# Layer 1's modulation as two-column products on TensorE beside the last attention heads

## The chip, the cores and the metric

One core of a Trainium2 chip. The metric is the device time of one execution in microseconds: 2973.62 us, the median of 3 runs (2972.55 to 2975.34). The engines are TensorE (PE, with its weight loads as PEld), VectorE (DVE), ScalarE (ACT), GpSimd (POOL) and SyncE (SP), which issues all DMAs of this kernel.

## What is computed

Two layers of a trunk over 1024 prompt tokens and 64 sample tokens, 1024 features. Layer 0 mixes with retention and differential attention, layer 1 with band attention and a state-space scan; each layer ends in a gated feed-forward network. What the change touches is the modulation: six vectors of 1024 values per layer and sequence (two sequences, prompt and sample), which scale, shift and gate the rest.

```python
c_act = jax.nn.silu(c)
for l in range(DEPTH):
    mod = c_act @ w_mod[l] + b_mod[l]                 # 1024 x 6144 per layer, fp32
    sh1, sc1, g1, sh2, sc2, g2 = jnp.split(mod, 6)    # one pair of columns: prompt, sample
    h = rmsnorm(x, norm_g[l, 0]) * (1.0 + sc1) + sh1
    ...                                               # attention and retention or scan -> out
    x = x + g1 * out
    h = rmsnorm(x, norm_g[l, 1]) * (1.0 + sc2) + sh2
    ...                                               # feed-forward -> f
    x = x + g2 * f
```

## The kernel before

The program is written in Tile: a planner orders each engine's instructions from the order of the program (earlier ones have priority) and its own model of when they are ready; pools hand out buffers by tag. The large products use fp32r, two halves (hi, lo) of each operand, three products each, and the stages follow one another: layer 0's projections and heads (to about 660 us), output product and norm, up products with the gate (line L648, about 799 to 1228), down products (L804, 1228 to 1513), then the same of layer 1 (heads to about 2140, up 2259 to 2683, down from 2683).

A layer's modulation is cut into 24 units of 256 output columns. Units 0 to 3 are the shift, 4 to 7 the scale and 8 to 11 the gate of the first half of the layer, 12 to 23 the same for the feed-forward half. Each has 1 MB of weights. Layer 0's units are made at the start and beside its retention. Layer 1's units are made by `mod_steps1` (L440): per unit four loads of 256 KB (L447), 16 ACT products (L453) that scale 128x256 weights with a per-partition value, 7 DVE sums of 128x512 (L455), then in `mod_sum` (L409) four transposes on TensorE and a DVE reduction (L411). Units 0 to 6 run in the up products of layer 0, from column block `f` = 4 on (the fifth of 22), where each block makes two of the five steps of a unit; units 7 to 19 in the down products of layer 0, one step each 1.6 tiles, with the rest finished ahead of the last pass; units 20 to 23 in the up products of layer 1. The class `Modulation` counts these steps. In the up products the side work's tiles (`mh`) come from the same 8 buffers as the tiles of the gate.

In the heads, `weave` (L1175) runs one head's attention and, between its steps, steps of `fill` (the projection of the next head, or in the last head the output product on the first half of the features, `early_out`, L1437) and of `side`. The last head of each layer first issues the loads of the output weights (`load_cols`, L188) and of the finished heads (`load_mixed`, `mxl`, L1575), then its attention. These loads, the projections' weights and all later weights use one tag `raw` with two buffers; the split halves have two buffers each as well (`wsp`). The products' banks `gs` are two, shared by projections, `early_out` and the first tiles of the next stage. The rest of the side work is finished after the last head, and then comes `block_tail` with the output products (`ops`) on the second half of the features, the norm, and the feed-forward network.

`nps` (L297) is a sum of squares over the partitions by TensorE, from `rstd_bcast`: for each of 3 column groups, 2 products of a 128x128 fp32 block with one column of ones.

Of the kernel before, what the change touches and what calls it, by code (L numbers as in the profile page):

```python
# [50 lines left out]
FS = 1.6  # L51
MHB = 3
MU = (7, 20, 24)
NPRE = 8
MS0 = 4
# [87 lines left out]
def build(ctx, tc, A, O, stop=None):  # L143
# [296 lines left out]
    def mod_steps1(l, units, pp, stage):  # L440

        for u in units:
            src = mod_src(l, u)
            acc = None
            for j0 in range(0, KT, 2):
                rv = stage()[:, :512].rearrange("p (j n) -> p j n", n=256)
                SY.dma_start(out=rv, in_=src[:, j0:j0 + 2, :])  # L447
                yield
                acc = acc or sm.tile([P, 2, 256], F32, tag="macc", name="macc", bufs=1)
                for j in range(j0, j0 + 2):  # L450
                    pr = acc if j == 0 else stage()[:, :512].rearrange("p (j n) -> p j n", n=256)
# [229 lines left out]
    def ffn_up(l, hv, pp, w, tmp, side, last):  # L681
# [12 lines left out]
        for f in range(NF):  # L694
# [33 lines left out]
            if f >= MS0:  # L728
                side.step()
# [33 lines left out]
            if f >= MS0:  # L763
                side.step()
# [28 lines left out]
    def ffn_down(l, x, gate, pp, yp, before, after, side, part0, xres):  # L793
        def tile(js, c, m, parts):
# [22 lines left out]
            side.step()  # L817

        for js in PASSES:
            if js[-1] == NPAIR - 1:  # L820
                before()
# [796 lines left out]
    for h in range(4):  # L1618
# [14 lines left out]
        weave(diff_attention(h, qk_.pop(h), vv_.pop(h), *late), iter(()) if late else fill, DW[h], mside, MS[1])  # L1633
# [5 lines left out]
    mod_scale(0, 1)  # L1639
    sta.close()  # L1640

    def block_tail(l, wout, am, nxt, side, wts):
# [4 lines left out]
        with ExitStack() as st:  # L1647
# [22 lines left out]
            with ExitStack() as su:  # L1670
# [3 lines left out]
                side.start(mod_steps1(1, range(MU[0]) if l == 0 else range(MU[1], MU[2]), pp, lambda: w("mh", F32)), 1)  # L1674
# [4 lines left out]
                ffn_up(l, hv, pp, w, lambda: up_.tile([P, 512], F32, tag="s2", name="s2", bufs=1), side, last)  # L1679
# [14 lines left out]
        def before():  # L1694
            side.end()
            if l == 0:
                mod_scale(1, 0)
                mod_scale(1, 1)
# [540 lines left out]
```

## Time and profile before

| | us |
|---|---|
| median of 3 runs | 2973.62 |
| the profiled execution | 2973.83 |
| its span, first to last instruction | 2972.1 |
| TensorE products busy | 2804.1 (94%) |
| TensorE weight loads busy | 2707.4 (91%) |
| VectorE busy | 1954.3 (66%) |
| ScalarE busy | 1296.3 (44%) |
| GpSimd busy | 787.3 (26%) |
| mean granted TensorE clock | 0.979 |

The span is 2972.1 us; what lies around it is 1.7 us. Busy time of TensorE's products is modelled and overlaps, so the share of its weight loads is the better measure of its idle time. Time runs from the span's start in all views. PEclk is the granted share of full clock, so 0.5 is 1.2 GHz and 1.0 is 2.4 GHz.

### The profile page before, as it was taken

How to read it: one execution, taken by the hardware profiler on the slowest of the kernel's cores; microseconds unless marked ns; L12 is line 12 of the kernel's file. 1: busy time of each engine (PE TensorE's matmuls, PEld its weight loads, DVE VectorE, ACT ScalarE, POOL GpSimd, SP SyncE). 2: the span in 40 equal slices, each digit the busy share in tenths (PEclk: the TensorE clock that was granted, in tenths of full speed). 3: DMA queues.
4: the chain of work that ended last, by engine and by line, in shares of the span. 5: the costliest groups of instructions: out<-in, count | busy, mean ns of one | idle time of the engine just before them, and what ended most of it. 6: DMA issues, size and time to landing. Idle time of an engine off the chain costs nothing.

```text
span 2972.1 us, 51195 instructions
## 1 busy us (share of the span) xinstructions
PE 2804.1 (94%) x19418; PEld 2707.4 (91%) x19418; DVE 1954.3 (66%) x4095; ACT 1296.3 (44%) x2938; POOL 787.3 (26%) x842
## 2 busy tenths in 40 slices
PE   7999999889999999999988999997999999999998
PEld 4999998779899999999988998986998999999997
DVE  5788766654788666587876675456268888764544
ACT  4221265644535444555552335556255454334111
POOL 4332222222255444412342352111100000004131
PEclk9999999889999999999989999999999999999999
DMA  7444421135544333553422331113344533235221
GB/s 241 139 131 142 126 62 60 46 98 159 158 130 137 91 101 96 183 173 128 138 82 74 86 98 50 52 55 93 99 132 144 153 101 102 71 98 184 90 81 61
DMA packets 351069, 330.53 MB, mean 111 GB/s; under 512 B 24898, under 2 KB 307047, under 8 KB 350823
## 3 DMA queue, kind: packets, MB, share of 16 engines
q1 hardware_dynamic: 350823, 327.26, 35.7%
q8 instruction: 153, 2.51, 0.4%
q14 instruction: 93, 0.76, 0.1%
HBM read 248.46 MB, written 78.73 MB: 110 GB/s over the span
## 4 chain that ended last, share of the span: by engine, by line
PE 47%; DVE 9%; DMA 6%; ACT 4%; issue 2%; POOL 1%; SPq 0%; DVEq 0%; ACTq 0%; POOLq 0%
PE dps L804 10%; PE pa L648 7%; PE pe L648 6%; PE pb L648 6%; DMA mh<-in_w_mod 3%; PE py L648 3%; PE qkps L231 3%; PE pvps L2110 2%; DMA raw<-in_w_up 2%; DVE macc L455 1%; ACT mh L453 1%; PE ops L231 1%; PE xps L231 1%; DVE wlo L596 1%; PE ptps L1316 1%
## 5 line engine op out<-in xcount | busy, mean ns | idle before, releaser
L804 PE MATMUL dps<-y,whi 128*128 128x384 f32 (+1 forms) x2112 | 518.8, 330 | 5.9 <-DVE sthi L160 4.2
L804 PEld LDWEIGHTS dps<-y,whi 128*128 128x128 f32 x2112 | 376.0, 189 | 7.2 <-DVE sthi L160 4.7
L595 ACT CAST whi<-raw 128x512 fp32r<-128x512 f32 x328 | 194.7, 617 | 372.4 <-PE pb L648 95.0
L804 PE MATMUL dps<-y,wlo 128*128 128x384 f32 (+1 forms) x1056 | 347.1, 330 | 0.0
L199 POOL TENSOR_TENSOR wlo<-raw,whi 128x2048 fp32r<-128x2048 f32 (+2 forms) x40 | 180.7, 4518 | 373.5 <-ACT whi L198 290.3
L160 DVE SCALAR_TENSOR_TENSOR x<-dps,modT,x 128x384 f32<-128x384 f32 (+1 forms) x320 | 149.4, 495 | 110.7 <-PE dps L804 110.1
L596 POOL TENSOR_TENSOR wlo<-raw,whi 128x512 fp32r<-128x512 f32 x116 | 162.1, 1402 | 208.1 <-ACT whi L595 203.1
L648 PE MATMUL pe<-row,whi 128*128 128x272 f32 x1056 | 205.9, 288 | 0.0
L804 PEld LDWEIGHTS dps<-y,wlo 128*128 128x128 f32 x1056 | 199.7, 189 | 0.0
L596 POOL TENSOR_TENSOR y<-y 128x544 fp32r<-128x544 f32 x88 | 133.0, 1543 | 250.4 <-ACT y L595 250.4
L453 ACT ACTIVATE mh<-mh,cact 128x256 f32<-128x256 f32 x336 | 145.8, 498 | 120.9 <-DMA mh<-in_w_mod 105.8
L455 DVE TENSOR_TENSOR macc<-macc,mh 128x512 f32<-128x512 f32 x168 | 142.7, 849 | 76.9 <-ACT mh L453 64.9
L596 DVE TENSOR_TENSOR wlo<-raw,whi 128x512 fp32r<-128x512 f32 x212 | 148.4, 718 | 64.1 <-ACT whi L595 63.4
L648 PE MATMUL pa<-row,whi 128*128 128x272 f32 x896 | 174.7, 292 | 10.3 <-ACT gs L669 10.3
L231 PE MATMUL qkps<-hhi,whi 128*128 128x384 f32 (+1 forms) x528 | 178.6, 342 | 3.3 <-DVE q L1383 2.0
L231 PE MATMUL qkps<-hlo,whi 128*128 128x384 f32 (+1 forms) x528 | 173.5, 332 | 0.0
L648 PEld LDWEIGHTS pe<-row,whi 128*128 128x128 f32 x1056 | 165.9, 188 | 0.0
L648 PE MATMUL pb<-bt,whi 128*128 128x272 f32 x816 | 156.8, 288 | 1.1 <-DVE u L717 1.1
L648 PE MATMUL pa<-bt,whi 128*128 128x272 f32 x768 | 151.0, 292 | 5.0 <-DVE row L160 3.1
L648 PEld LDWEIGHTS pa<-row,whi 128*128 128x128 f32 x896 | 143.1, 192 | 11.0 <-ACT gs L669 11.0
L648 PE MATMUL pe<-row,wlo 128*128 128x272 f32 x528 | 152.4, 289 | 0.0
L648 PE MATMUL py<-bt,whi 128*128 128x272 f32 x704 | 136.1, 290 | 4.0 <-ACT whi L595 2.4
(462 smaller groups left out, 8077.2 us busy)
## 6 DMA issues: line engine op xcount, KB each, us to landing
raw<-in_w_up SPq DMA_DIRECT2D x104, 512.0 KB
mh<-in_w_mod SPq DMA_DIRECT2D x96, 256.0 KB
yd<-e SPq DMA_DIRECT2D x88, 272.0 KB
y<-yd SPq DMA_DIRECT2D x44, 544.0 KB
raw<-in_w_down SPq DMA_DIRECT2D x22, 1024.0 KB
mq<-in_w_mod SPq DMA_DIRECT2D x64, 256.0 KB
raw<-in_w_in_ab SPq DMA_DIRECT2D x24, 512.0 KB
xr<-xspill SPq DMA_DIRECT2D x32, 193.0 KB
```

Of the source, the lines that this page charges most:

```text
L160: V.scalar_tensor_tensor(out=out, in0=in0, scalar=scalar, in1=in1, op0=op0, op1=op1, **kw)
L199: eng.tensor_tensor(out=lo[:, sl], in0=raw[:, sl], in1=hi[:, sl].bitcast(F32), op=ALU.subtract)
L231: T.matmul(out=ps[:, b:n], lhsT=lt, rhs=rh, start=(i == 0), stop=(i == len(mms) - 1))
L453: S.activation(out=pr[:, s, :], in_=rv[:, j - j0, :], func=AF.Copy, scale=cact[:, j, s:s + 1])
L455: V.tensor_add(acc, acc, pr)
L595: S.copy(hi, src)
L596: eng.tensor_tensor(out=lo, in0=src, in1=hi.bitcast(F32), op=ALU.subtract)
L648: T.matmul(out=ps[t], lhsT=lt, rhs=rh, start=(first and i == 0), stop=(i == len(mms) - 1), skip_group_check=not first)
L804: T.matmul(out=ps[:, :n], lhsT=lt, rhs=rh, start=(i == 0), stop=(i == len(mms) - 1))
L1316: T.transpose(ps[:kk, P * (b - b0):P * (b - b0 + 1)], e[:, P * b:P * b + kk], ident)
L2110: T.matmul(out=ps[:, :P], lhsT=pts[m][:kk, b, :], rhs=vv[:kk, :], start=(b == 0), stop=(b == nb - 1))
```

## The change

Layer 1's units are no longer made in the feed-forward stages. `mod_steps1`, the class `Modulation` and its calls in `ffn_up` and `ffn_down` go away. A new `mod_cols` makes a unit in two steps: one load of 1 MB into a `raw` buffer; then 16 products, 8 for each half of the 256 columns, with a 128x128 block of the weights as the stationary operand and the two columns of `cact` as the moving one, summed in a `gs` bank, and the DVE sum with the bias. Units 0 to 3 run as side steps of layer 0's third head, 4 to 7 of its last head, 8 to 11 of layer 1's third head and 12 to 23 of its last head. The number of side steps per step of `fill` is set for each head (`MS1`, `MS2`), and what is left is finished after the last head. `mod_scale` of layer 1 moves to the ends of these stages.

```diff
+MA = ((0, 0), (0, 0), (0, 4), (4, 8))
+MS1 = (1.0, 1.0, 0.33, 0.07)
+MC = ((8, 8), (8, 8), (8, 12), (12, 24))
+MS2 = (0.0, 0.0, 0.3, 0.62)
...
-    def mod_steps1(l, units, pp, stage):
+    def mod_cols(l, units, pp):
         for u in units:
-            src = mod_src(l, u)
-            acc = None
-            for j0 in range(0, KT, 2):
-                rv = stage()[:, :512].rearrange("p (j n) -> p j n", n=256)
-                SY.dma_start(out=rv, in_=src[:, j0:j0 + 2, :])
-                yield
...
-                    for s in range(2):
-                        S.activation(out=pr[:, s, :], in_=rv[:, j - j0, :], func=AF.Copy, scale=cact[:, j, s:s + 1])
-                    if j:
-                        V.tensor_add(acc, acc, pr)
+            raw = wrp.tile([P, WU], F32, tag="raw", name="rawm")
+            rv = raw[:, :2048].rearrange("p (j n) -> p j n", n=256)
+            SY.dma_start(out=rv, in_=mod_src(l, u))
             yield
-            mod_sum(l, u, pp.tile("t", "mps"), [acc[:, s, :] for s in range(2)])
+            ps = pp.tile("g", "mps")
+            for b in range(2):
+                for j in range(KT):
+                    T.matmul(out=ps[:, 2 * b:2 * b + 2], lhsT=rv[:, j, P * b:P * b + P], rhs=cact[:, j, :], start=(j == 0), stop=(j == KT - 1))
+            mod_bias(l, u, ps)
+            yield
...
-            if f >= MS0:
-                side.step()
...
-            side.step()
...
+        mside = chain(mside, mod_cols(1, range(*MA[h]), pm))
+        weave(diff_attention(h, qk_.pop(h), vv_.pop(h), *late), iter(()) if late else fill, DW[h], mside, MS1[h])
...
     mod_scale(0, 1)
+    mod_scale(1, 0)
...
+        mside = chain(mside, mod_cols(1, range(*MC[pr]), pm))
+        weave(band_attention(pr, qk_.pop(pr), vv_.pop(pr), *late), iter(()) if late else fill, BW[pr], mside, MS2[pr])
...
+    for _ in mside:
+        pass
+    mod_scale(1, 1)
```

## Rows read from the trace of the kernel before

**Rows 1.** The page: chain that ended last by line; two groups (busy us, mean ns | idle)
```profile
PE dps L804 10%; PE pa L648 7%; PE pe L648 6%; PE pb L648 6%; DMA mh<-in_w_mod 3%; PE py L648 3%; PE qkps L231 3%; PE pvps L2110 2%; DMA raw<-in_w_up 2%; DVE macc L455 1%; ACT mh L453 1%; PE ops L231 1%; PE xps L231 1%; DVE wlo L596 1%; PE ptps L1316 1%
...
L453 ACT ACTIVATE mh<-mh,cact 128x256 f32<-128x256 f32 x336 | 145.8, 498 | 120.9 <-DMA mh<-in_w_mod 105.8
L455 DVE TENSOR_TENSOR macc<-macc,mh 128x512 f32<-128x512 f32 x168 | 142.7, 849 | 76.9 <-ACT mh L453 64.9
```

**Rows 2.** Stretches: length, PE and PEld busy (count), PEclk, DMA share, GB/s; L804, then L648
```profile
1228.00:1461.50 233.50, 219.42 (x1296) 215.77 (x1297) 0.99 0.50 162
2683.40:2898.00 214.60, 214.60 (x1297) 214.44 (x1298) 1.00 0.34 118
...
799.00:1228.00 429.00, 420.44 (x3312) 416.97 (x3312) 1.00 0.38 116
2259.50:2683.40 423.90, 417.64 (x3312) 415.23 (x3312) 1.00 0.36 110
```

**Rows 3.** Waits of TensorE (us, times, longest), 1228 to 1515, then 860 to 934
```profile
PE mps L409 <- DVE macc L455: 9.4, 7, 2.6
PE dps L804 <- DVE e L160: 1.0, 1, 1.0
...
PE py L648 <- DVE m L411: 1.5, 1, 1.5
...
PE pb L648 <- DVE u L717: 0.7, 1, 0.7
```

**Rows 4.** Stretches of heads: length, PE, PEld, DVE, ACT, POOL busy (count), PEclk, DMA, GB/s
```profile
480.00:620.00 140.00, 114.10 (x662) 99.78 (x660) 102.22 (x299) 92.02 (x240) 39.90 (x73) 0.93 0.18 54
620.00:660.00 40.00, 36.02 (x216) 34.15 (x217) 15.11 (x36) 11.72 (x34) 7.10 (x19) 0.88 0.32 103
660.00:740.00 80.00, 78.43 (x477) 77.50 (x476) 31.88 (x72) 27.85 (x64) 17.14 (x10) 1.00 0.52 149
1868.00:1980.00 112.00, 108.30 (x788) 103.28 (x787) 47.66 (x122) 57.07 (x162) 13.29 (x19) 1.00 0.18 53
1980.00:2065.00 85.00, 67.94 (x423) 58.90 (x423) 51.74 (x134) 52.78 (x154) 13.45 (x11) 0.94 0.27 77
2065.00:2072.00 7.00, 5.18 (x39) 4.38 (x37) 6.31 (x17) 6.40 (x18) 2.16 (x2) 1.00 0.62 210
2072.00:2200.00 128.00, 124.44 (x798) 120.69 (x796) 51.18 (x118) 44.43 (x113) 17.18 (x10) 1.00 0.37 106
```

**Rows 5.** Instructions of tile nps (ns min/median/max), then timeline of weight loads from 707.86
```profile
L297 PEld LDWEIGHTS nps<-ones,nacc x108: 187/192/334, 702.0 to 2211.0; 128*128 128x128 f32 x108
...
L300 DVE TENSOR_SCALAR r<-nps x9: 147/160/161, 708.9 to 2211.4; 128x3 f32<-128x3 f32 x9
...
707.77 0.97 PEld L297 LDWEIGHTS nps<-ones,nacc 128*128 128x128 f32 x8
```

**Rows 6.** Timeline of SP's issues (start, us), 600 to 624, then 2045 to 2066
```profile
606.40 8.33 SPq L1575 DMA_DIRECT2D mxl<-mixd  x4
618.91 3.05 SPq L188 DMA_DIRECT2D raw<-in_w_out_ab  x2
...
2049.23 0.33 SPq L1421 DMA_DIRECT2D mixd<-ot  x1
...
2051.91 0.90 SPq L1575 DMA_DIRECT2D mxl<-mixd  x2
...
2061.53 0.36 SPq L1575 DMA_DIRECT2D mxl<-mixd  x1
2065.18 0.37 SPq L188 DMA_DIRECT2D raw<-in_w_out_cd  x1
```

**Rows 7.** One stretch of a head; weight loads of L804 after 1305.7 and after 1310
```profile
2040.00:2060.00 20.00, 15.46 (x85) 12.11 (x83) 9.01 (x34) 11.84 (x39) 1.28 (x5) 0.83 0.46 137
...
L804 PEld LDWEIGHTS dps<-y,whi x8: 311/334/334, 1305.6 to 1308.8; 128*128 128x128 f32 x8
...
L804 PEld LDWEIGHTS dps<-y,whi x60: 187/188/188, 1309.8 to 1325.0; 128*128 128x128 f32 x60
```

More of the change, by code (lines that the diff above doesn't have):

```diff
@@ L679, in ffn_pre, with ffn_up @@
             yield
-    def ffn_up(l, hv, pp, w, tmp, side, last):
+    def ffn_up(l, hv, pp, w, tmp, last):
         raw = up_raw(l, 0)
@@ L791, in down_w, with ffn_down @@
         return [t[:, :2048].rearrange("p (k n) -> p k n", n=512) for t in (hi, lo)]
-    def ffn_down(l, x, gate, pp, yp, before, after, side, part0, xres):
+    def ffn_down(l, x, gate, pp, yp, after, part0, xres):
         def tile(js, c, m, parts):
@@ L1639, in build, with block_tail @@
     mod_scale(0, 1)
+    mod_scale(1, 0)
     sta.close()
-    def block_tail(l, wout, am, nxt, side, wts):
+    def block_tail(l, wout, am, nxt, wts):
         def work(pool_, width, n):
@@ L1678, in last @@
                     part0.append(([load_y(l, 0), load_y(l, 1)], down_w(l, PASSES[0], 0)))
-                ffn_up(l, hv, pp, w, lambda: up_.tile([P, 512], F32, tag="s2", name="s2", bufs=1), side, last)
-                side.end()
+                ffn_up(l, hv, pp, w, lambda: up_.tile([P, 512], F32, tag="s2", name="s2", bufs=1), last)
         st = ctx.enter_context(ExitStack())
@@ L1690, in block_tail @@
         ffn_state(l, pp)
-        if l == 0:
-            side.start(mod_steps1(1, range(MU[0], MU[1]), pp, lambda: fp.tile([P, 512], F32, tag="mh", name="mh", bufs=MHB)), FS)
[L1694 to L1698, printed above, removed]
-        ffn_down(l, x, gate_of(l, 1), pp, fp, before, lambda c: nxt(c, x, pp, lambda name, dt=F32: w(name, dt)), side, part0[0], lambda: w("xr", F32))
+        ffn_down(l, x, gate_of(l, 1), pp, fp, lambda c: nxt(c, x, pp, lambda name, dt=F32: w(name, dt)), part0[0], lambda: w("xr", F32))
         return st
@@ L1717, in to_layer1 @@
         x_spill(x, c)
-    class Modulation:
-        gen, n, every = None, 0, 1
-        def start(self, gen, every):
-            self.gen, self.n, self.every = gen, 0, every
-        def step(self):
-            self.n += 1
-            while self.gen is not None and self.n >= self.every:
-                self.n -= self.every
-                next(self.gen, None)
-        def end(self):
-            for _ in self.gen or ():
-                pass
-            self.gen = None
-    block_tail(0, A["w_out_ab"][0], am, to_layer1, Modulation(), wts).close()
+    block_tail(0, A["w_out_ab"][0], am, to_layer1, wts).close()
     a = acts1["h"]
@@ L2169, in build @@
             fill = early_out(am, gate_of(1, 0), wts, fm, pm, ready)
-        weave(band_attention(pr, qk_.pop(pr), vv_.pop(pr), *late), iter(()) if late else fill, BW[pr])
+        mside = chain(mside, mod_cols(1, range(*MC[pr]), pm))
+        weave(band_attention(pr, qk_.pop(pr), vv_.pop(pr), *late), iter(()) if late else fill, BW[pr], mside, MS2[pr])
         if late:
```

15 lines of the change are left out of this document (1 added, 14 removed).

## The prediction

> **What bounds the kernel now.** The chain of waits comes first: TensorE's products hold most of the line shares, with one foreign streak, the side work of the modulation (loads of mh 3%, macc and mh 1% each) [rows 1]. The feed-forward stages of the two layers are then the same work with and without much of that side work, so they are laid side by side. The down products of layer 0 need 233.5 us for 1296 products, those of layer 1 214.6 us for the same 1296, and in layer 1 weight loads fill the whole stretch [rows 2]: TensorE is the bound there, and in layer 0 something is in its way. The waits of TensorE name it: seven transposes that waited for macc, 9.4 us [rows 3]. The up products differ by less, 429.0 against 423.9 us [rows 2], with one unit of side work every two and a half columns in layer 0.
>
> The attention stages are the place where the work goes. There I read weight loads (PEld) and not matmuls as TensorE's fill, since matmuls overlap. Idle by that measure: 40.2 us of 480 to 620, 5.9 us of 620 to 660, 2.5 us of 660 to 740; in layer 1 8.7 us of 1868 to 1980, 26.1 us of 1980 to 2065, 2.6 us of 2065 to 2072 and 7.3 us of the 128 us after that [rows 4]. So the heads have idle time, but it ends at about 660 and 2072, when the output products (ops) begin and TensorE is the bound again.
>
> **What the change removes.** Of the 24 units of layer 1, 13 ran in the down products of layer 0, 7 in its up products, 4 in those of layer 1. Each had 16 ACT products, 7 DVE sums and 4 transposes. The down products of layer 0 should come to layer 1's pace: 233.5 - 214.6 = 18.9 us. I take 18, since a first wait (DVE e, 1.0 us [rows 3]) is not the side work's. What is late next there is TensorE itself. The up products of layer 0: four waits in columns 5 to 8, the longest 1.5 us and the shortest 0.7, 4.6 us together [rows 3], lie in the stretch with side work, the longest of them on its reduction outright, and 28 transposes take 28 x 0.11 = 3.1 us (spaced as the weight loads of rows 5). Together at most 7.7; I take 6. Layer 1's: 16 transposes, 1.8 us, and part of its own waits; 3. ACT (498 ns) and DVE (849 ns) [rows 1] are freed of some 330 us, which by itself is worth nothing where TensorE is the bound. **Gain 27 us, ends 20 and 33.**
>
> **What it adds.** Per unit one 1 MB load into a raw buffer, 16 products of a 128x128 weight block in plain fp32 with two columns, one small DVE sum. The nearest operation in the trace is nps (L297): 128x128 fp32 weights, one column. It shows 108 loads for 9 sums of squares [rows 5]; the code issues 3 x 2 products for each, 54 in all, so one fp32 product is two load-and-multiply pairs. Eight loads in a row take 0.97 us with 0.19 us for the last: (0.97 - 0.19) / 7 = 0.111 us from one to the next [rows 5]. A unit is 16 x 2 x 0.111 = 3.55 us of TensorE, 24 units 85.2 us. The columns hardly count; the weight loads do.
>
> The Trainium skill (TensorE: Matmul & The Clock Gate, Back-to-back issue gap) gives about 25 ns from start to start for up to 64 columns, and for loading 128 columns of weights 107 ns (LDWEIGHTS). The trace's 0.111 us agrees with the second; by the first alone a unit would be an estimated 32 x 0.025 = 0.8 us, all 24 units 19 us, which the idle time of the heads would hide nearly whole, and the sum would be some 2950.
>
> **Where it falls, four groups.** Products run in the planner's fixed order, so idle time hides them only where the load is early and the buffers are free.
> - Units 0 to 3 (14.2 us, layer 0's third head): raw buffers free well before; 40.2 us idle [rows 4]. Cost 0 to 14.2; I take 3, near the idle end.
> - Units 4 to 7 (14.2 us): their buffers come after the loads of mxl, which in the trace are issued at 606.4 to 614.7 and wait for the third head's result; the next raw load is at 618.9 [rows 6]. From there 5.9 + 2.5 = 8.4 us are idle [rows 4], and the last unit stands behind the output products by program order. Cost 5.8 to 14.2; I take 9.
> - Units 8 to 11 (14.2 us, layer 1's third head): 8.7 us idle, then 26.1 [rows 4]. Cost 0 to 14.2; I take 4.
> - Units 12 to 23 (42.6 us, layer 1's last head): the same order of buffers decides. mxl for the second chunk waits until 2051.9 for the mixd store at 2049.2, another mxl load that needs nothing new is issued only together with it, the last is at 2061.5 and the next raw load at 2065.2 [rows 6]. Units 12 to 23 stand behind these, so they begin at 2065 at the earliest, and the 26.1 us before that are lost to them. Left are 2.6 + 7.3 = 9.9 us [rows 4]. Cost 32.7 to 42.6; I take 37.
>
> Sum 53 us. The queue of SP: a modulation load that waits for its buffer holds back the loads behind it (caches, xe, rows of the residual); with two buffers that is at most a unit's product time, 3.55 us, and costs nothing while the cached keys of the sample tile have landed early; if not, it costs the same few us once per head. The loads are 12 MB in the 128 us after 2072, 94 GB/s on top of 106 [rows 4]; 2065 to 2072 moved 210 [rows 4], so I cost them at nothing. The output weights are loaded later, but their buffers for the split come free only when the first ones are used up, so nothing waits. The sums of units 8 to 11 are needed by the output products of the last head, and are done by then.
>
> **The clock.** In 2040 to 2060 the mean granted clock was 0.83, with weight loads in 12.1 of 20 us [rows 7]; at 1.2 GHz a weight load of dps takes 334 ns, at 2.4 GHz 188 [rows 7]. In 1305.6 to 1308.8 the fall followed a wait of TensorE (2.6 us, the longest of the seven [rows 3]). No row shows what a long run of two-column products does. If units 12 to 23 run at 0.83, they need 42.6 / 0.83 - 42.6 = 8.7 us more; at 1.0 nothing; at 1.2 GHz throughout 42.6 more. I take 8, nearest to the row of the same kind of stage.
>
> **Sum.** The profiled execution took 2973.83 us, 2972.1 of it span, and the median is 2973.62, so both bases agree. 2973.8 - 27 + 53 + 8 = 3008.
>
> **Rivals.**
> - Clock: the two-column products leave TensorE at 1.2 GHz through layer 1's last head. For it: the heads' stretches are those with a mean under 1 (0.93, 0.88, 0.94 [rows 4]). Against it: the output products have 1.00. 42.6 in place of 8: 3043.
> - The other side: the raw buffers are handed out as they come free and not in program order. Place: 1980 to 2065. Then 26.1 us more are open to units 12 to 23, they cost 42.6 - 36.0 = 6.6 and keep the clock up, and units 4 to 7 start earlier as well (3): 3 + 3 + 4 + 6.6 - 27 = -10, 2963. It decides from the point where units 12 to 23 cost under 27 - 16 = 11 us, clock included, that is, where 32 of their 42.6 us are hidden. Against it: the mxl load that waited without need [rows 6].
> - The gain isn't there: another limit takes the place in layer 0's down products, and only transposes are saved, 24 x 4 x 0.11 = 11: 3024.
> - Weight loads hide under each other: then a product costs its two columns, 2/384 of a dps product (214.6 / 1296 = 0.166 us [rows 2]), which is nothing, and only some 3 us of single waits stand against the gain: 2950. Against it: the spacing of nps [rows 5].
>
> **How the numbers follow.** Forecast 0.60 (its own range 2985 to 3032), clock 0.16, other side 0.10, no gain 0.10, cheap loads 0.04. Low end of all terms: 38.5 of cost less 33, 2979; high end of the costs 85.2 less 20, with 8 of clock, 3047. I set 2978 to 3050, which leaves out most of the other side, cheap loads and the tail of the clock. A measurement of this kernel can tell about 0.2% (6 us) from no change. Faster by more: cheap loads and over half of the other side, 0.10; within: the rest of it and the forecast's lowest end, 0.06; slower 0.84.
>
> **What would show it.** Down products of layer 0 at 215 us to the 1296th, with no wait for macc. For the new mps products 768 weight loads, 0.111 us apart. First load of a unit in layer 1's last head not before 2061 (as counted in the old trace), and output products that start some 40 us later against the last mxl. The granted clock of that head: under 0.83 speaks for the first rival. Loads of unit 12 before the last mxl, or weight loads spaced 25 ns, would make me wrong; so would down products that stay above 225 us.

## The result and the profile after

The changed kernel takes 3103.39 us, the median of 4 runs (3097.12 to 3106.99), against 2974.14 us for the kernel before beside it: a ratio of 1.0432, with a 95% interval of 1.0416 to 1.0449. Slower, as forecast, but by 129 us where 34 were forecast, and outside the range. The profiled execution took 3097.12 us, 123.3 more than that of before, with a span of 3095.3 us and a mean granted clock of 0.950 (0.979 before).

The gain came as forecast. These are the stretches of [rows 2] in the changed kernel (length, PE and PEld busy with counts, PEclk, DMA share, GB/s): first 1296 down products of layer 0 and of layer 1 (line L795 now), then the up products of both layers (L643).

```profile
1268.70:1483.20 214.50, 214.50 (x1296) 214.34 (x1297) 1.00 0.35 120
2806.60:3021.20 214.60, 214.60 (x1297) 214.44 (x1298) 1.00 0.34 118
...
849.00:1268.70 419.70, 416.96 (x3312) 416.10 (x3312) 1.00 0.33 101
2385.90:2806.60 420.70, 417.49 (x3312) 417.00 (x3312) 0.99 0.32 101
```

Layer 0's down products fell from 233.5 to 214.5 us, its up products from 429.0 to 419.7, layer 1's from 423.9 to 420.7. Together 31.5 us. The whole loss, and these 31.5 us with it, must then lie mostly in the heads.

They can be laid side by side by their work, from the start of the third head (its load of tn or tb) to the start of the fourth, and from there to the first gate product. First layer 0, then layer 1; length, PE, PEld, DVE, ACT, POOL busy, PEclk, DMA share, GB/s. The kernel before:

```profile
505.10:584.10 79.00, 65.99 (x395) 59.78 (x394) 54.78 (x138) 49.50 (x124) 25.40 (x37) 0.96 0.17 51
584.10:737.30 153.20, 138.96 (x804) 130.68 (x805) 74.82 (x201) 64.61 (x170) 35.24 (x51) 0.92 0.42 125
1977.90:2049.70 71.80, 58.08 (x382) 51.91 (x381) 43.81 (x102) 42.21 (x121) 10.90 (x10) 0.98 0.23 64
2049.70:2197.40 147.70, 140.54 (x882) 133.43 (x881) 64.31 (x159) 59.32 (x159) 21.89 (x12) 0.98 0.40 117
```

The changed kernel:

```profile
504.00:585.10 81.10, 76.35 (x498) 73.08 (x496) 47.02 (x144) 45.70 (x120) 14.60 (x34) 0.87 0.28 86
585.10:787.40 202.30, 173.07 (x959) 164.88 (x959) 81.42 (x207) 69.92 (x174) 45.55 (x54) 0.82 0.40 122
1997.80:2087.10 89.30, 78.22 (x498) 71.83 (x497) 41.65 (x106) 45.53 (x123) 15.49 (x11) 0.85 0.34 107
2087.10:2324.20 237.10, 226.81 (x1278) 220.16 (x1277) 70.58 (x171) 60.00 (x160) 21.89 (x12) 0.79 0.43 132
...
2087.00:2206.00 119.00, 111.14 (x583) 105.97 (x584) 32.86 (x98) 32.14 (x91) 4.72 (x2) 0.63 0.40 130
```

and of these the products of the units alone (L450; PE and PEld busy, PEclk):

```profile
504.00:585.10 81.10, 16.45 (x128) 16.91 (x128) 0.87 0.28 86
585.10:787.40 202.30, 21.63 (x128) 22.05 (x128) 0.82 0.40 122
1997.80:2087.10 89.30, 16.04 (x128) 16.47 (x128) 0.85 0.34 107
2087.10:2324.20 237.10, 67.92 (x384) 69.09 (x384) 0.79 0.43 132
```

By stretch the cost is 2.1, 49.1, 17.5 and 89.4 us, 158.1 in all. The idle time of TensorE is the length less PEld: 75.9 us in the four stretches before, 79.8 after. **Taken together, none of it was filled.** In layer 0's third head it fell from 19.2 to 8.0 us, but in layer 0's last head it rose from 22.5 to 37.4. There TensorE waits for the pass over the scores that finds the row maximum (mx), first before, then after (total us, times, longest):

```profile
PE sps L1364 <- DVE mx L1304: 1.2, 3, 0.5
...
PE sps L1352 <- DVE mx L1292: 15.1, 9, 3.7
```

The other 154 us are busy time: the units' own weight loads, 124.5 us in the four stretches (85.2 is the bare price), and 29.6 us more for the same loads as before. What exceeds the bare price goes with the lower clock: it is 0.79 to 0.87, and 0.63 in the 119 us in which most of units 12 to 23 are made.

The weight loads of the units (ns min/median/max), by their tile:

```profile
L450 PEld LDWEIGHTS mps<-cact,rawm x768: 186/192/370, 528.8 to 2253.0; 128*128 128x128 f32 x192
```

and in the timeline (start, us), once in layer 0's third head and once in layer 1's last:

```profile
528.77 2.98 PEld L450 LDWEIGHTS mps<-cact,rawm 128*128 128x128 f32 x26
...
2131.74 6.95 PEld L450 LDWEIGHTS mps<-cact,rawm 128*128 128x128 f32 x32
```

There are 768 loads. At full clock they come (2.98 - 0.19) / 25 = 0.112 us apart, the forecast's price; in layer 1's last head a unit takes 6.95 us in place of 3.6. TensorE also has a new wait, between 700 and 760 us (total, times, longest): the output product on the second half of the features waits for its weights.

```profile
PE ops L216 <- ACT whi L198: 7.5, 1, 7.5
```

SP's issues show why (start, duration). First the first output weights in the kernel before, in each layer:

```profile
419.11 0.38 SPq L188 DMA_DIRECT2D raw<-in_w_out_ab  x1
...
1868.73 0.37 SPq L188 DMA_DIRECT2D raw<-in_w_out_cd  x1
```

and in the changed kernel, with the first load of unit 12 as the last line:

```profile
570.14 0.38 SPq L188 DMA_DIRECT2D raw<-in_w_out_ab  x1
...
733.62 0.38 SPq L188 DMA_DIRECT2D raw<-in_w_out_ab  x1
...
2046.24 0.38 SPq L188 DMA_DIRECT2D raw<-in_w_out_cd  x1
...
2099.03 0.36 SPq L1563 DMA_DIRECT2D mxl<-mixd  x1
...
2102.68 0.55 SPq L445 DMA_DIRECT2D rawm<-in_w_mod  x1
```

The first output weights come 151 and 178 us later (in layer 1, 20 us of this is that the whole head lies later). The two further ones of layer 0, both issued from 618.9 on before [rows 6], go out at 660.2 and 733.6. All stand behind the units' loads in the two raw buffers. With that `early_out` begins at 660 and 2206 us in place of 559 and 2013.

### The profile page after: what moved, and what is told of

Its sections match the earlier page's. It is cut to its first block, busy times and chain, and to the rows that moved or that the text cites. A ratio compares the mean times of both kernels' runs of the same rounds, so it can differ in the third digit from the quotient of the medians.

```text
span 3095.3 us, 51702 instructions
## 1 busy us (share of the span) xinstructions
PE 2939.7 (95%) x20090; PEld 2852.8 (92%) x20090; DVE 1808.1 (58%) x3903; ACT 1144.8 (37%) x2554; POOL 774.3 (25%) x842
## 4 chain that ended last, share of the span: by engine, by line
PE 80%; DVE 8%; DMA 4%; ACT 3%; issue 3%; POOL 1%; SPq 1%; DVEq 0%; POOLq 0%; ACTq 0%
PE dps L795 17%; PE pe L643 9%; PE pa L643 8%; PE qkps L231 7%; PE pb L643 7%; PE py L643 4%; PE mps L450 3%; PE ops L231 2%; PE pvps L2072 2%; PE xps L231 2%; PE ptps L1304 1%; PE ops L216 1%; DVE macc L160 1%; PE ops L217 1%; PE pvps L1499 1%
## 5 line engine op out<-in xcount | busy, mean ns | idle before, releaser
L795 PE MATMUL dps<-y,whi 128*128 128x384 f32 (+1 forms) x2112 | 517.5, 329 | 4.3 <-DVE sthi L160 4.3
L795 PEld LDWEIGHTS dps<-y,whi 128*128 128x128 f32 x2112 | 375.1, 189 | 5.4 <-DVE sthi L160 4.7
L795 PE MATMUL dps<-y,wlo 128*128 128x384 f32 (+1 forms) x1056 | 345.6, 329 | 0.0
L643 PE MATMUL pe<-row,whi 128*128 128x272 f32 x1056 | 208.0, 291 | 0.0
L795 PEld LDWEIGHTS dps<-y,wlo 128*128 128x128 f32 x1056 | 199.2, 189 | 0.0
L591 POOL TENSOR_TENSOR y<-y 128x544 fp32r<-128x544 f32 x88 | 124.4, 1448 | 242.8 <-ACT y L590 242.7
L643 PE MATMUL pa<-row,whi 128*128 128x272 f32 x896 | 173.1, 290 | 9.2 <-ACT gs L664 9.2
L643 PEld LDWEIGHTS pe<-row,whi 128*128 128x128 f32 x1056 | 168.0, 191 | 0.0
L643 PE MATMUL pa<-bt,whi 128*128 128x272 f32 x768 | 151.2, 292 | 6.0 <-DVE row L160 4.2
L643 PE MATMUL pb<-bt,whi 128*128 128x272 f32 x816 | 156.6, 288 | 0.0
L643 PE MATMUL pe<-row,wlo 128*128 128x272 f32 x528 | 153.6, 291 | 0.0
L643 PEld LDWEIGHTS pa<-row,whi 128*128 128x128 f32 x896 | 142.2, 191 | 10.1 <-ACT gs L664 10.1
L198 ACT CAST whi<-raw 128x2048 fp32r<-128x2048 f32 (+2 forms) x43 | 76.6, 1789 | 180.9 <-PE dps L795 90.3
L643 PE MATMUL py<-bt,whi 128*128 128x272 f32 x704 | 134.3, 288 | 2.4 <-ACT whi L590 2.4
L643 PE MATMUL pa<-row,wlo 128*128 128x272 f32 x448 | 129.8, 290 | 0.0
```

Source lines behind the costliest of these rows:

```text
L198: S.copy(hi[:, sl], raw[:, sl])
L591: eng.tensor_tensor(out=lo, in0=src, in1=hi.bitcast(F32), op=ALU.subtract)
L643: T.matmul(out=ps[t], lhsT=lt, rhs=rh, start=(first and i == 0), stop=(i == len(mms) - 1), skip_group_check=not first)
L795: T.matmul(out=ps[:, :n], lhsT=lt, rhs=rh, start=(i == 0), stop=(i == len(mms) - 1))
```

## The experiments

Three things could carry the loss: the clock, the order of the heads (loads, buffers and banks that the units take from others), and the bare price of products that no idle time hides. Single executions of the kernel before, beside these runs, lay between 2965 and 2986 us, so differences under some 15 us between single runs are not read; stretches of one trace are steadier (without units or other edits in them, the third heads and layer 1's last head repeat within about 1 us from kernel to kernel, layer 0's last head within about 4, and whole stages elsewhere move by up to 6 us).

| run | us | clock | what it is |
|---|---|---|---|
| before | 2974 | 0.979 | |
| after | 3103 | 0.950 | two columns, changed places |
| e1_wide | 3044.73 | 0.973 | 128 columns, changed places |
| e2_last | 3099.13 | 0.951 | two columns, units of the last heads behind early_out |
| e3_wide_last | 3057.52 | 0.977 | both |
| e4_none | 2927.72 | 0.982 | no units |
| f1_bank | 3082.59 | 0.971 | 128 columns, other banks |
| f2_spread | 3011.03 | 0.981 | 128 columns, units in the first two heads |
| f3_delay | 2973.62 | 0.979 | before, transposes one step later |
| g1_third | 3023.84 | 0.979 | 128 columns, four units in each third head |
| g2_narrow | 3050.92 | 0.968 | two columns, first two heads |
| h2_wfirst | 3022.23 | 0.977 | g1 with early output weights |
| h3_flip | 3060.00 | 0.971 | operands swapped, changed places |
| i1_late | 2984.27 | 0.980 | before, with late output weights |
| j1_dummy3 | 2991.50 | 0.982 | before, with empty units in the third heads |
| j2_dummy4 | 3007.45 | 0.981 | before, with empty units in the last heads |
| k1_loads | 2971.36 | 0.976 | e1 with 2 of 16 products of a unit |

### Clock or order: e1_wide, e2_last, e3_wide_last, e4_none

The moving operand of a unit's product gets 128 columns, of which two are read afterwards:

```diff
-    cact = cp.tile([P, KT, 2], F32, name="cact")
+    cwide = cp.tile([P, 16 + P], F32, name="cwide")
+    cact = cwide[:, :16].rearrange("p (j s) -> p j s", s=2)
...
-T.matmul(out=ps[:, 2 * b:2 * b + 2], lhsT=rv[:, j, P * b:P * b + P], rhs=cact[:, j, :], start=(j == 0), stop=(j == KT - 1))
+T.matmul(out=ps[:, P * b:P * b + P], lhsT=rv[:, j, P * b:P * b + P], rhs=cwide[:, 2 * j:2 * j + P], start=(j == 0), stop=(j == KT - 1))
```

> The changed kernel, but each modulation product streams 128 columns in place of 2 (the first two are the real ones, the rest of the moving operand is later columns of the same vector and zeros). The weight loads, 0.111 us apart at full clock, stay the bound of a product, so its price at 2.4 GHz is the same 3.55 us a unit; banks, buffers and order are the same. Theory A (clock: two-column products leave TensorE at 1.2 GHz): granted clock of both last heads over 0.95, mean pitch of the weight loads 0.11 us, some 45 to 75 us less than the changed kernel, about 3040. Theory B (the bank order holds early_out behind the units): no change, within 8 us of 3103. Theory C (it is the bare price of the products, 85 us): no change either.

3044.73 us. Theory A's time holds: the same weight loads, buffers and places, and 59 us less than the median of after (52 less than its profiled execution). Its clock of over 0.95 in both last heads came in layer 1's only; layer 0's has 0.87 (0.92 before the change). The four stretches, as above, and the first part of the last one, with most of units 12 to 23:

```profile
507.00:582.80 75.80, 68.77 (x495) 66.10 (x493) 49.05 (x142) 44.19 (x118) 14.76 (x34) 0.99 0.26 83
582.80:779.60 196.80, 161.26 (x963) 152.53 (x962) 85.29 (x211) 71.70 (x176) 44.69 (x54) 0.87 0.43 129
1987.00:2077.50 90.50, 74.00 (x499) 67.97 (x497) 48.62 (x106) 45.93 (x123) 15.46 (x11) 0.87 0.34 106
2077.50:2273.60 196.10, 185.59 (x1277) 179.92 (x1277) 67.23 (x172) 59.84 (x160) 21.85 (x12) 0.97 0.53 158
...
2077.50:2157.00 79.50, 72.68 (x582) 68.31 (x582) 33.33 (x98) 31.89 (x92) 4.72 (x2) 0.98 0.60 190
```

559.2 us together, 50.6 less than after, 41.0 of it in layer 1's last head, whose clock rose from 0.79 to 0.97. But 559.2 is still 107.5 more than before, over the bare 85.2, and idle time is now 92.7 us. So the clock is one cause and not the larger one.

Units of the last heads behind `early_out` in program order, with two columns:

```diff
-MS1 = (1.0, 1.0, 0.33, 0.07)
-MS2 = (0.0, 0.0, 0.3, 0.62)
+MS1 = (1.0, 1.0, 0.33, 0.0)
+MS2 = (0.0, 0.0, 0.3, 0.0)
```

> The changed kernel, but no side steps in the two last heads: units 4 to 7 and 12 to 23 come after early_out in program order, so the two gs banks no longer hold early_out behind them. Theory A (clock): the units then run close together with little between them, at 1.2 GHz, 7.1 us each, 16 x 7.1 = 114 us nearly all exposed, less what early_out gives back by running in idle time (some 40 to 60 us): 3060 to 3110. Theory B (bank order): early_out starts where it did before the change (about 560 and 2015) and its overlap comes back, the units cost 16 x 3.55 = 57 us: about 3005. Theory C: no change, 3103.

3099.13 us, 94 from theory B's time. `early_out` starts 65 and 116 us sooner than in the changed kernel, but at 595 and 2090 us, not at the 560 and 2015 that theory B names; so the order as such is tested only in part. Nothing is won: the units, now without attention around them, run at half clock (the weight loads of all units have a median of 333 ns).

> Both edits, 128 columns and units of the last heads after early_out. Theories A and B together: 3010 to 3030 (gain of the feed-forward stages 31 us against 57 us of units after the heads at full clock plus some 15 us of the others). Theory A alone: the same as with 128 columns only, about 3040. Theory B alone: the same as with the order only, about 3005. Theory C: 3103.

3057.52 us, no better than e1_wide and above what A and B together gave. In layer 1 the units now stand in a row and wait for their own loads: TensorE waited 16.4 us for rawm in 2143 to 2240.

e4_none leaves the making of layer 1's modulation out and sets it to a constant (`MA` and `MC` all empty), to show what any placing could gain at most.

> The changed kernel with layer 1's modulation left out (its 24 units and their loads aren't made, a constant stands in their place). This is the ceiling: all theories expect the feed-forward stages' gain and nothing else, 2974 less 31 = 2943; up to 10 us more or less would say that the units also move other work of the heads by the planner's order.

2927.72 us, 15 less than all theories expected. All side work of layer 1's modulation cost 46 us in the kernel before, and costs 169 in the changed one (by its profiled execution).

### Order: f1_bank, f2_spread, g2_narrow

```diff
-            ps = pp.tile("g", "mps")
+            ps = pp.tile("t", "mps")
```

> The changed kernel with 128 moving columns (as in e1_wide) and, besides, the units' sums in the two banks of the attention's own transposes (tag t) in place of the two banks that the output products of the last head use too. Theory O (order of the banks): in the heads the idle time of TensorE is not filled because each unit pushes a part of the early output products (early_out) out of it: both want the same two banks in program order. Without that the early output products start again near 595 us in layer 0 (655 in e1_wide) and near 2020 in layer 1 (2157), and the time falls from 3045 to 3020 to 3035. Theory R (the raw buffers and SP's queue): the early output products wait for their own weights and rows, which stand behind the units' loads; then they start late as before, the wait of 12.8 us for the second output weights stays, and the time stays within 3040 to 3050. Theory C (nothing in the heads can be hidden, since the idle time is the attention's own chain of waits): early output products earlier, time unchanged, 3040 to 3050.

3082.59 us, worse than all three expected. `early_out` did start earlier (610 and 2096 us, against 655 and 2157), but the idle time of the four stretches went to 137.5 us. The units now share the banks of the attention's transposes, which is the likely reason, though not shown. This run says that these banks are no place for the units; it can't decide on theory O.

```diff
-MA = ((0, 0), (0, 0), (0, 4), (4, 8))
+MA = ((0, 4), (4, 8), (8, 8), (8, 8))
-MS1 = (1.0, 1.0, 0.33, 0.07)
+MS1 = (0.3, 0.3, 0.33, 0.07)
...
-MC = ((8, 8), (8, 8), (8, 12), (12, 24))
+MC = ((8, 16), (16, 24), (24, 24), (24, 24))
-MS2 = (0.0, 0.0, 0.3, 0.62)
+MS2 = (0.6, 0.6, 0.3, 0.62)
```

> The changed kernel with 128 moving columns, and with units 0 to 7 moved to the first two differential heads of layer 0, 8 to 23 to the first two band heads of layer 1, so that the last two heads of both layers have none. Theory R and O together: from the third head's start to the first gate product each layer is back at the length of before, 232 us and 220 us (in e1_wide 273 and 287), and what is left is the bare price of the products, 24 x 3.55 = 85 us, less at most the idle time of the first two heads (3.4 + 7.3 us in layer 0, 9.2 + 8.3 in layer 1, measured without any units): 2928 + 85 - (0 to 28) = 2985 to 3013. Theory C: place doesn't matter, since nothing was hidden anywhere and nothing was lost to the order: 3035 to 3050. Against both: units in the first heads push the projections' weights back through the two raw buffers, and the time goes above 3050.

3011.03 us, inside 2985 to 3013, at its high end. The last stretches of the layers are those of before again:

```profile
605.90:756.80 150.90, 134.30 (x804) 127.63 (x805) 75.66 (x201) 64.26 (x170) 35.64 (x51) 0.94 0.44 127
...
2089.60:2237.10 147.50, 140.45 (x883) 133.40 (x881) 64.33 (x159) 59.37 (x159) 21.89 (x12) 0.98 0.40 118
```

So the places of the change cost 34 us with 128 columns (3045 - 3011), and away from them the units cost 3011 - 2928 = 83 us, their bare price of 85: nothing is hidden in the first heads, which have little idle time.

> f2_spread with the two moving columns of the changed kernel in place of 128; units 0 to 7 in the first two differential heads of layer 0, 8 to 23 in the first two band heads of layer 1. There TensorE is busy with the projections' 384-column products (PEld 96% and 98% of two of these heads with units). Theory P (the clock falls where two-column products meet a head without other long products): granted clock of these heads above 0.95, time 3005 to 3020. Theory A (the two-column products pull the clock down wherever they stand): granted clock of these heads 0.65 to 0.9 and 25 to 60 us more, 3035 to 3070.

3050.92 us, theory A: the clock is lost there too. The second band head of layer 1, with ten units' loads in each stretch, in f2_spread and in this kernel:

```profile
1888.00:2008.50 120.50, 120.40 (x958) 118.01 (x957) 37.12 (x112) 45.68 (x132) 9.96 (x9) 1.00 0.39 120
```

```profile
1917.00:2052.00 135.00, 132.82 (x929) 129.76 (x928) 41.15 (x112) 44.84 (x130) 10.94 (x13) 0.87 0.33 100
```

TensorE's weight loads fill 96% and more of both, yet with two columns the clock is 0.87 (the other loads are 29 fewer in the second stretch). The four runs make a square: 128 columns save 52 us at the changed places and 40 at the others; the other places save 46 with two columns and 34 with 128.

### Can the idle time be filled: g1_third, h2_wfirst, i1_late, j1_dummy3, j2_dummy4, k1_loads

> Like f2_spread (128 moving columns, none in the last heads), but four units of each layer are put into the third head: 0 to 3 in the first two differential heads, 4 to 7 in the third; 8 to 19 in the first two band heads, 20 to 23 in the third. The third heads have 19.4 and 19.6 us of idle TensorE without any units. Theory I (this idle time can be filled, and the changed kernel lost by what it pushed out of the last heads): the eight units of the third heads are hidden, the time falls from 3011 by up to 28 us, to 2983 to 2997. Theory N (idle time of the heads is the attention's own chain of waits and products, and a unit costs its bare 3.55 us wherever it stands): 3005 to 3018. Theory R (units in the third head take the raw buffers that the last head's weights need, and early_out starts some 35 us late, as in e3): the last head is longer by 10 us or more per layer and the time is 3020 to 3045.

3023.84 us, in theory R's range, but only 6 us above theory N's, which single runs don't tell apart. By the stretches, layer 0's third head was filled (75.2 us; 79.1 in f2_spread without units there) and its last head grew by 20.6 us, as theory R has it; in layer 1 the third head grew by 11.6 us and the last by 0.5, which is not theory R. The first output weights went out at 587 us. h2_wfirst brings them forward:

```diff
             wts = [load_cols(A["w_out_ab"][0], 256 * u) for u in range(2)]
+            for _ in mod_cols(1, range(4, 8), pm):
+                pass
             load_mixed(am, MXA)
```

and the same with units 20 to 23 in layer 1.

> g1_third with one thing changed: the four units of each third head (4 to 7; 20 to 23) are issued behind the first output weights of the last head and ahead of its rows (mxl), in place of ahead of both. In the kernel before those weights are issued at 419 and 1869 us, in the changed kernel at 570 and 2046, in g1_third at 587 and 2066. Theory R (the units take the raw buffers that the output weights need, so early_out starts late and is missing as filler): the weights are issued within 540 us, early_out begins in layer 0 near 581 us as in f2_spread (612 in g1_third), the last head of layer 0 is back from 171.5 to about 151 us, and the time is 2985 to 3008. Theory F (early_out already fills what can be filled; units in the third head push it out whatever the buffers do): early_out as late as in g1_third, idle time of all heads together stays at 100 to 110 us, and the time is 3010 to 3030.

3022.23 us. The weights were issued at 485 and 505 us, and little was won: layer 0's last head came back from 171.5 to 162.2 us (theory R: 151), the four stretches from 487.4 to 479.5, the whole not beyond noise. The rows of the finished heads (mxl) now stood behind the units' loads, first at 593 us. Theory R's time falls; theory F's holds, but not yet its reason. i1_late tests that alone, on the kernel before:

```diff
-            wts = [load_cols(A["w_out_ab"][0], 256 * u) for u in range(2)]
             load_mixed(am, MXA)
+            wts = [load_cols(A["w_out_ab"][0], 256 * u) for u in range(2)]
```

> The kernel before (units in the feed-forward stages as they were), with two lines of each last head swapped: the first output weights are loaded behind the rows of the finished heads (mxl) and not ahead of them. No unit, no two-column product and no work is added; the weights just come some 150 us later, as they do in the changed kernel (419 and 1869 us before, 570 and 2046 after). It measures alone what it costs to take early_out out of the third head and the first part of the last one. Theory F (early_out is the filler of these heads; without it TensorE idles and the same products run after the heads): early_out begins after 600 us in layer 0 and after 2060 in layer 1, idle time from the third head to the first gate product goes from 42 + 34 us to 85 to 105 together, and the time goes to 2982 to 3010. Rival (the idle time is the attention's own, and early_out is only shifted within it): the time stays within 2970 to 2979.

A ratio of 1.0029 (1.0014 to 1.0043), 8.5 us by the medians. The time of 2984 lies at the low end of theory F's range, but the idle time of 85 to 105 us does not come. In the profiled execution (2976 us, the fastest of the ten) `early_out` began at 619 and 2065 us, 60 and 52 us later than before, and the four stretches together are as before, 451.6 us with 75.9 idle:

```profile
sum 451.60, PE 402.81 PEld 375.68 DVE 229.89 ACT 217.11 POOL 99.60; mean PE 100.70 PEld 93.92 DVE 57.47 ACT 54.28 POOL 24.90
```

So **`early_out` some 55 us late costs TensorE nothing in the heads** of this execution. Where the 8.5 us of the medians lie, it doesn't show. In the changed kernel `early_out` is 101 and 193 us late; theory F falls for the shorter delay and stays open for that one.

j1_dummy3 and j2_dummy4 put products of the units' kind into the kernel before, on constants, so without loads and with no reader:

```diff
+    def dummy(n, pp):
+        for u in range(n):
+            ps = pp.tile("g", "dmy")
+            for b in range(2):
+                for j in range(KT):
+                    T.matmul(out=ps[:, P * b:P * b + P], lhsT=ident, rhs=cwide[:, 2 * j:2 * j + P], start=(j == 0), stop=(j == KT - 1))
+            yield
+            yield
...
+        mside = chain(mside, dummy(NDC[pr], pm))
```

> The kernel before, with its own units in the feed-forward stages as they were, and besides four empty units in the third head of each layer: 16 fp32 products each, 128x128 stationary and 128 moving columns like e1_wide, but of constants that lie in SBUF, so with no load, no raw buffer and no reader. 8 x 3.55 = 28.4 us of TensorE; the third heads have 19.3 and 19.9 us of idle time. Theory N (the idle time lies in waits of TensorE's fixed order, and products put in beside them add their bare price): 2995 to 3010. Theory L (it could be filled, and what spoilt it were the units' loads in the raw buffers and SP's queue): 2972 to 2985.

> The same with the empty units where the changed kernel has its last sixteen: four in the last head of layer 0, twelve in the last head of layer 1; no loads. 16 x 3.55 = 56.8 us, or less if the last few of layer 1 find no step of the head (the count of products tells). Theory N: bare price, 15.5 us less for each four units missing; 3025 to 3040 with all of them, with clock above 0.95. Theory L: the idle time of the last heads (22.4 and 14.1 us) takes a part, 2995 to 3015. Theory O (banks): the empty units take turns in the banks of early_out and hold it back as in e1_wide; then layer 0's last head alone is longer by 25 us or more, where bare price is 14.2.

2991.50 us is between the theories, 3007.45 us in theory L's range. Other stages moved too, so the stretches tell more. j1_dummy3:

```profile
507.70:589.00 81.30, 75.07 (x518) 71.53 (x516) 52.33 (x139) 49.06 (x122) 24.72 (x37) 0.98 0.17 50
...
1991.50:2066.30 74.80, 69.28 (x507) 64.20 (x505) 38.96 (x102) 42.51 (x121) 10.91 (x10) 1.00 0.22 61
```

j2_dummy4:

```profile
506.60:593.20 86.60, 78.08 (x523) 73.87 (x522) 56.48 (x142) 50.20 (x126) 25.44 (x39) 0.96 0.16 47
593.20:742.10 148.90, 134.39 (x805) 127.09 (x805) 70.85 (x198) 63.90 (x166) 34.94 (x50) 0.95 0.44 128
1989.30:2079.10 89.80, 84.31 (x667) 81.01 (x666) 43.41 (x102) 42.15 (x121) 10.95 (x10) 1.00 0.18 51
2079.10:2231.70 152.60, 148.29 (x981) 143.11 (x980) 65.01 (x159) 59.27 (x159) 21.89 (x12) 1.00 0.39 114
...
L470 PEld LDWEIGHTS dmy<-cwide,ident x384: 187/192/213, 2024.2 to 2093.8; 128*128 128x128 f32 x192
```

In j1 the third heads are 2.3 and 3.0 us longer than before, not 14.2 each, and half of their idle time is gone (9.8 and 10.6 us left of 19.2 and 19.9). All four stretches are 459.0 us in j1 and 477.9 in j2, 7.3 and 26.2 over before, for products of 28.4 and 56.8 us. **Idle time can be filled**: it falls by 12.9 us in j1 and 23.1 in j2, and the other loads take 9.5 and 11.5 us less, at a clock that is mostly a little higher. Theory N falls. The starts show how: units that need no load are taken ahead into the third heads (j2's 12 units run from 2024 to 2094 us, the last line), where the idle time is; the changed kernel's units 12 to 23 start at 2111, behind their loads. Both kernels draw on the same third heads, so their gains can't simply be added: all 24 empty units in one kernel were not tried. By the whole time the two cost 16.5 and 32.4 us.

k1_loads keeps all loads of e1_wide and 2 of a unit's 16 products; layer 1's modulation is left incomplete.

```diff
-                for j in range(KT):
+                for j in range(1):
```

> e1_wide with all 24 loads at their places and only two of each unit's sixteen products (the first block of rows), so layer 1's modulation is left incomplete and its time is that of the loads and their buffers: 24 x 2 pairs x 2 x 0.111 = 11 us of products are left of 85. Without any units the kernel takes 2928 us, with loads and products 3045; products without loads cost 33 us in these heads where their bare price is 85 (j1_dummy3 and j2_dummy4: 7.6 us in layer 0, 25.7 in layer 1). Theory L (the loads in the raw buffers and SP's queue cost by themselves: late output weights, late mxl, early_out after the heads): 2970 to 3000. Theory X (loads alone are cheap, and it is a product that waits for its load and stands in TensorE's order ahead of the attention that costs): 2930 to 2955.

2971.36 us, at the low end of theory L. Over e4_none that is 43.6 us, 10.7 of them products. So loads alone cost at most 33 us. The four stretches are 474.9 us long against 446.7 in e4_none, with the products left in them; the rest lies in other stages. First e4_none, then k1_loads:

```profile
sum 446.70, PE 400.12 PEld 372.50 DVE 236.45 ACT 215.41 POOL 93.98; mean PE 100.03 PEld 93.12 DVE 59.11 ACT 53.85 POOL 23.50
...
sum 474.90, PE 417.63 PEld 388.28 DVE 241.83 ACT 219.64 POOL 97.16; mean PE 104.41 PEld 97.07 DVE 60.46 ACT 54.91 POOL 24.29
```

The products left out make up the rest of e1_wide: 73.4 us, against a bare price of 74.6.

The square is then: no units 2928; loads alone about 33 more; products alone 34 in the heads (j1 and j2 added, so a low bound); both together 117. Neither cost is that large by itself. That the loads hold the products back until the idle time has passed, so that every product is paid in full, fits units 12 to 23. It doesn't fit units 8 to 11: the loads of 8 and 9 go out 109 and 66 us ahead of their head, and yet nothing is hidden there. Which of the things behind the loads does most of it (mxl, the second output weights, a product that waits in TensorE's order) was not separated further: the two runs that moved one of them each, f1_bank and h2_wfirst, moved another one with it. A version with buffers of its own for the units wasn't tried.

### The other form, and the gain: h3_flip, f3_delay

```diff
-            for b in range(2):
-                for j in range(KT):
-                    T.matmul(out=ps[:, 2 * b:2 * b + 2], lhsT=rv[:, j, P * b:P * b + P], rhs=cact[:, j, :], start=(j == 0), stop=(j == KT - 1))
+            for j in range(KT):
+                T.matmul(out=ps[:2, :256], lhsT=cact[:, j, :], rhs=rv[:, j, :], start=(j == 0), stop=(j == KT - 1))
...
+            V.tensor_copy(row[:2, :], ps[:2, :256])
...
+                T.transpose(pt[:, 2 * b:2 * b + 2], row[:2, b * P:(b + 1) * P], ident[:2, :2])
```

> The changed kernel with the operands of its products swapped: the two columns of cact are the stationary operand, 256 columns of weights the moving one, 8 products a unit, then a DVE copy of the 2 x 256 row and two transposes into columns. The kernel before makes some units of layer 0 in this form at its start, with 0.216 us from one load-and-multiply pair to the next, 16 pairs or 3.45 us a unit, so the price is that of the changed kernel's 32 pairs (3.55 us), but with long moving streams. Theory A (what pulls the clock down is the narrow moving side, not the unit's place or its weight loads): granted clock of layer 1's last head above 0.95, time as e1_wide or a little above, 3040 to 3065, the rest for transposes that wait for the copy. Rival (any fp32 product of this size there takes the clock along): clock below 0.85, 3085 to 3115. Third: the second bank that each unit takes costs more than the clock gives: clock above 0.95 and yet 3070 or more.

3060.00 us, theory A. In layer 1's last head up to `early_out` the clock is 0.96, with weight loads in only 56% of the time:

```profile
2084.60:2167.00 82.40, 76.70 (x425) 45.76 (x424) 35.08 (x102) 30.04 (x86) 4.71 (x2) 0.96 0.60 189
```

f3_delay issues the transposes of a unit one step later, in the kernel before.

```diff
             yield
-            mod_sum(l, u, pp.tile("t", "mps"), [acc[:, s, :] for s in range(2)])
+            fin = (u, acc)
```

> The kernel before, with the four transposes and the sum of each unit of layer 1 issued one step later (behind the next unit's first load). Measures what the gain of 19 us in layer 0's down products consisted of. If it was TensorE's wait for macc (seven waits, 9.4 us), the waits go away, the 1296 down products take 224 to 226 us in place of 233.5, and the whole is 2963 to 2968. If the waits only show a side work whose pace was too slow (ACT and DVE behind), they stay with one step more, and the time is within 2970 to 2977. If the wait moves to the buffers of the side work, 2974 or more.

A ratio of 0.9988 (0.9976 to 1.0000), the second expectation: no gain to be told from none. The waits for macc in layer 0's down products stay, 8.5 us in 8 where they were 9.4 in 7 [rows 3]. So what the 19 us of gain in layer 0's down products consist of isn't shown by a run; half of it has the size of these waits.

## Why the prediction was wrong, point by point

- **The direction and the gain were right.** 27 us was the sum for the feed-forward stages, 31.5 came: 19.0 for layer 0's down products (18 taken), 9.3 for its up products (6), 3.2 for layer 1's (3). What the 19.0 us were lost to, the waits for macc or the rest, stays argued (f3_delay).
- **The price of a product was right**: 0.112 us a load by the rows above, 0.111 forecast. The Trainium skill (TensorE: Matmul & The Clock Gate, Back-to-back issue gap) gives 25 ns for products alone, and lets both operations set the spacing in a stream of weight loads and products. The trace agrees with the second, since here each product brings new weights.
- **The idle time as cover was wrong, and this is the step that failed most.** The groups with 128 columns (e1_wide, whose clock is 0.87 in the middle two), against the terms: units 0 to 3 -3.2 us (3 taken), 4 to 7 43.6 (9), 8 to 11 18.7 (4), 12 to 23 48.4 (37): 107.5 in place of 53. Part of the first two is a shift: 29 loads of `early_out` moved from layer 0's third head into its last. The sum took the idle time of [rows 4] as space that a unit fills if its load is early. The space is there (empty units took 12.9 us of it in j1 and 23.1 in j2), but with the loads only units 0 to 3 found it. The other three groups cost more than their bare 14.2, 14.2 and 42.6 us. The units' loads push the others' loads back; how much each of these costs stays open.
- **"So nothing waits" was wrong.** The forecast let the later output weights go at zero, and SP's queue at zero or a few us. The first output weights went out 151 and 178 us later, the last ones of layer 0 came at 733.6, and TensorE stood 7.5 us for them (12.7 in e1_wide). Loads alone cost up to 33 us.
- **The order of the loads in layer 1's last head was right**: unit 12 is loaded 3.7 us after the last mxl, so the rival of raw buffers out of order falls. Its consequence was mis-sized: after that point nothing is hidden, where 5.6 us were taken off. The output products on the second half of the features start 154 us after the last mxl (2253.3 against 2099.0) and before the change 61 us after it: 93 us later, where some 40 were named as a sign.
- **The clock was mis-sized**: 8 us for units 12 to 23 against 41 in their stretch and 52 in the whole kernel. The mechanism stood among the rivals, with 0.16, and its sign came: a clock of that head under 0.83 (0.79). Its time of 3043 was short by 54 us as well, mostly because it kept the cost of 53 us at full clock. The row taken as nearest, 0.83 in [rows 7], was a stretch without units; with them 0.63 came. Of the 69 us of busy time over the bare price, 39 are the units' own loads (124.5 - 85.2) and 30 the attention's and the output products' beside them (405.4 in place of 375.8), which no term held. (The 51 us that 128 columns save in the four stretches are less than these 69: e1_wide's own loads are 5 us over the bare price too, and it has 13 us more of idle time.)
- **The base**: without any units the kernel takes 2928 us, 19 less than 2973.8 - 27. Some 5 of these are a gain in the feed-forward stages above 27, the others lie in stages that the forecast left untouched.

As a sum: 2928 + 33 (loads) + 85 (products) + 52 (clock) = 3098; the profiled execution took 3097. This is no check of its own, since the terms are differences of the same runs; it only says where the time went.

## What to carry to other kernels

Idle time of an engine is not yet cover for work that has to be loaded first: the same products were hidden in part without their loads, and not with them. Ask for each moved product where its load stands in the queue, which buffer it takes, and whose load it pushes back. The cheapest test is a run with the same products on constants and a run with the loads alone. And before a product with two columns is put among others, try it with a wide moving side, by padding or by swapping the operands: here padding left a unit's price as it was (3.6 and 3.7 us), and the clock of layer 1's last head went from 0.79 to 0.97.

## What the runs showed of the hardware

- A stretch can be full of weight loads and still run for the most part at 1.2 GHz. In 2087 to 2206 us of the changed kernel weight loads took 105.97 of 119 us, and the granted clock was 0.63; with 128 columns and the same loads the same part of the head had 0.98 (2077.5 to 2157 in e1_wide).
- Not only the small products slow down: a unit went from 3.6 to 6.95 us in layer 1's last head, and the attention's and output products' loads beside them took 8% more in the four stretches together.
- A 128x128 fp32 product takes nearly the same 0.11 us per pair at full clock with 2 and with 128 moving columns, where each brings its own weights: 0.112 us by the rows above, and 44.7 / 384 = 0.116 in e1_wide's layer 1 last head (a unit 3.7 us).
